# A hybrid decoder block on one Trainium2 core: weights split in their own order, a ring that waits for whole quads only from expert 9, and the final norm's rows made at expert 22

## The chip, the cores and the metric

The kernel runs on one core of one Trainium2 chip. The metric is the device time of one launch in microseconds (us). The kernel before was timed three times: 1261.85, 1260.22 and 1263.72 us, median 1261.85. One execution more was profiled; its own time was 1259.29 us, and the span that the profiler shows of it 1257.5 us.

## The reference

The input is 256 tokens of width 1024; 16 learned meta tokens are put ahead of them. All is fp32.

```python
hn = rmsnorm(h, norm_mix)                                   # mixer
u, q, k, v, g_ssm, g_attn = split(hn @ w_in)                # 1024 1024 128 128 1024 1024
ssm_out = z * sigmoid(z @ w_glu + b_glu),  z = gelu(s5(u))  # diagonal recurrence, 64 groups x 64 states
attn_out = window_attention(rotary(q), rotary(k), v, sinks) # window 128, 16 heads, 2 kv heads
mix = sigmoid(g_ssm) * (ssm_out @ w_br_ssm) + sigmoid(g_attn) * (attn_out @ w_br_attn)
h = h + mix @ w_out
h = h + moe(rmsnorm(h, norm_ffn))                           # top 4 of 32 experts
return rmsnorm(h, norm_final)[:, 16:]
# moe, for each token and each of its 4 experts e, weighted by the softmax of the top-4 logits:
g, up = split(x @ w_gate_up[e] + b_gate_up[e])              # 1024 -> 2 x 1024
y = (min(g, 7) * sigmoid(1.702 * g) * (clip(up, -7, 7) + 1)) @ w_down[e] + b_down[e]
```

The weights of one expert are 12 MiB (8 of gate_up, 4 of down), so the 32 experts read 384 MiB from HBM.

## The kernel before

**Two halves.** The first 331 us are the mixer: the norm, the blocks of w_in, the recurrence, and then a loop over `n` (its body ends at L1265) in which 40 blocks of weights pass through a pipeline: `gate` (n 0 to 7), `glu`, `ssm`, `attn` and `out`, eight each. A block's weights (128 x 1024) are split in two parts: `hi` (L927, ACT) writes the high part `wh`, `lo` (L929 to L930, DVE or POOL) the rest `wl`; `mm` (L944 to L953, PE) multiplies three times; `e1` to `e4` work on the result. The 14 steps of the attention (maxima, exponentials, normalisation, transposes, values) are woven into the passes n = 0 to 13. The rest of the span is the router and the loop over the 32 experts `e` (L1552).

**The lists' order.** The experts' down weights and the residual `xt` use an order in which 512 columns, seen as 128 x 4, are turned to 4 x 128. `reorder(t, q)` (L903 to L906) turns a quarter of the residual, by two copies on POOL through a free piece of `late_`, at n = 3, 4, 5 and 6. The out blocks are split with a strided read (`self.p`, L924 to L930), and so come out in that order; `e2` (L974 to L979) adds the residual on DVE in PSUM and ACT copies the sum to `xt`; `e3` (L987) squares it; `turn_out` (L994 to L1002) turns it by eight matmuls with the identity, 64 wide, for the router. At the other end `down` (L1441 to L1442) evacuates PSUM with a strided read, `combine` (L1467) adds to `acc`, and `scale` (L1528 to L1529) turns the result back by strided operations on ACT and DVE.

**The ring.** The experts' weights come through `Ring` (L131 to L165), on SP's DMA queue. It owns slots of 1 MiB: four quads, which the trace names by the tile they lie in (`r`, `ZScgtX`, `QYWgt`, `ws`), and slots that stand alone (one in `r`, one in `aA`). A unit of work is 4 MiB; it goes out as one transfer to a whole free quad, as halves of 2 MiB, or as single slots. Slots come free when PE has used them, and each release calls `pump`. With `patient` set, a unit that has not begun waits for a whole quad and everything behind it waits too. That is set by one line in the loop over the experts:

```python
ring.patient, ring.most = 4 < e < 29, 4 if e < 29 else 2
```

**The end.** At the last expert ACT's queue loads the rows of `norm_final` (L1556) and PE spreads them over the partitions into two PSUM banks (`nf_banks`, L1508 to L1511), which `weigh` (L1524) and `scale` read; `squares` and `root` (L1516 to L1520) make the norm, and three of SP's transfers and one of ACT's write the output (L1531 to L1532).

Of the kernel before, what the change touches and what calls it, by code (L numbers as in the profile page):

```python
# [95 lines left out]
class Ring:  # L96
# [36 lines left out]
    def pump(self):  # L133
        while self.free and self.todo:
# [11 lines left out]
            row = self.room(4) if left == self.most else None  # L146
# [57 lines left out]
def hybrid_block(ctx: ExitStack, tc: tile.TileContext, x, meta, norm_mix, w_in, lam_re, lam_im, log_dt,  # L204
# [698 lines left out]
    def reorder(t, q):  # L903
        v, tmp = xt[:, t, 512 * q:512 * q + 512], late_[:, 3 * 512:]
        G.tensor_copy(tmp, v)
        G.tensor_copy(v.rearrange("p (c n) -> p c n", c=4), tmp.rearrange("p (n c) -> p c n", c=4))  # L906

    class Block:
# [5 lines left out]
        def hi(self):  # L914
# [48 lines left out]
        def e2(self):  # L963
# [10 lines left out]
            elif self.kind == "out" and self.h:  # L974
                pu = pus[self.i][:, :, :256].rearrange("p t (c n) -> p t c n", c=4)
                for t in range(2):
                    V.scalar_tensor_tensor(pu[:, t], pu[:, t], 0.5, strips(t, self.i), op0=OP.mult, op1=OP.add)
                for t in range(2):
                    S.activation(strips(t, self.i), pu[:, t], AF.Copy)  # L979
# [223 lines left out]
    for n in range(B + 2):  # L1203
# [33 lines left out]
        if 3 <= n < 7:  # L1237
            reorder((n - 3) // 2, (n - 3) % 2)
# [18 lines left out]
        if n == 22:  # L1257
            ring.slots([aA(8 * L + 768, U_)])
# [157 lines left out]

    cols2 = lambda t: t.rearrange("p (n c) -> p c n", c=4)
    rows2 = lambda t: t.rearrange("p (c n) -> p c n", c=4)

    def down(hT_, wc, selr, y, odd, mid=None, two=False):  # L1420
# [20 lines left out]
        S.activation(rows2(y[:64, odd]), cols2(py[0][:64]), AF.Copy)  # L1441
        V.tensor_copy(rows2(y[64:, 1 - odd]), cols2(py[1][64:]))  # L1442
# [18 lines left out]
    def combine(gT, y, then=None):  # L1461
        for t in range(2):
            for hf in range(2):
# [3 lines left out]
                V.tensor_tensor(acc[:, t, cs_], (acc if started else xt)[:, t, cs_], pc, op=OP.add)  # L1467
# [232 lines left out]
```

## Time and profile before

| what | before |
|---|---|
| median of three runs | 1261.85 us |
| the profiled execution, its span | 1259.29 us, 1257.5 us |
| PE busy | 1186.2 us (94%) |
| DVE, ACT, POOL busy | 461.9, 235.7, 65.0 us |
| bytes moved | 447.26 MB, mean 356 GB/s |
| chain that ended last | PE 64%, DMA 26%, DVE 7%, ACT 2% |

The chain is followed back from the last instruction, so its shares say which engine or transfer was waited for. The mean of 356 GB/s mixes a mixer that moves less than 240 GB/s over most of its time with experts at about 432. A row of the timeline gives the start, the duration, the engine, the line, the output and inputs, and in square brackets the idle time before it and what ended it.

### The profile page before, as it was taken

The numbers are of one execution on the slowest core, as the hardware profiler recorded it, in microseconds if no ns is written. First come the engines' busy times: TensorE is split into PE (matmuls) and PEld (weight loads), VectorE is DVE, ScalarE is ACT, GpSimd is POOL, SyncE is SP. The second block draws the span as 40 slices with busy tenths as digits, with TensorE's granted clock in tenths as the row PEclk, the third lists the DMA queues.
The fourth block names the chain that finished last, engine by engine and source line by source line (L and its number), as shares of the span: only waits on it lengthen the run. The fifth ranks groups of instructions, "written<-read, shape, count | busy, mean of one in ns | idle before, by whom it ended". The sixth has DMA issues, their size and how long they took to land.

```text
span 1257.5 us, 16838 instructions
## 1 busy us (share of the span) xinstructions
PE 1186.2 (94%) x7200; PEld 598.1 (48%) x7201; DVE 461.9 (37%) x1002; ACT 235.7 (19%) x478; POOL 65.0 (5%) x97
## 2 busy tenths in 40 slices
PE   8989979999899999999999989899998989999995
PEld 6878768899533333333333333333332333333331
DVE  4979467778421222322121212222231312121223
ACT  3353456647100000000000000000000000000002
POOL 3019130000000000000000000000000000000000
PEclk9999989999999999999999999999999999999998
DMA  7934345685889999999999999999999999999993
GB/s 181 238 84 140 131 149 170 135 318 208 366 358 431 427 430 386 433 433 433 432 432 433 431 432 433 432 430 432 432 433 432 431 432 433 430 431 432 426 430 146
DMA packets 76401, 447.26 MB, mean 356 GB/s; under 512 B 22377, under 2 KB 58461, under 8 KB 59937
## 3 DMA queue, kind: packets, MB, share of 16 engines
q1 hardware_dynamic: 75660, 445.40, 87.3%
q8 instruction: 59, 0.97, 0.3%
q0 software_dynamic: 512, 0.45, 0.2%
q10 hardware_dynamic: 148, 0.27, 0.1%
q14 instruction: 22, 0.17, 0.0%
HBM read 443.32 MB, written 2.79 MB: 355 GB/s over the span
## 4 chain that ended last, share of the span: by engine, by line
PE 64%; DMA 26%; DVE 7%; ACT 2%; issue 1%; POOL 0%; SPq 0%; DVEq 0%; ACTq 0%
PE pgt L1390 13%; PE pup L1390 11%; PE py L1435 11%; DMA ZScgtX<-in_w_gate_up_dram 10%; DMA r<-in_w_gate_up_dram 10%; PE pg L1363 6%; PE pc L1465 4%; PE pu L506 2%; DMA QYWgt<-in_w_gate_up_dram 2%; PE pu L951 2%; DMA r<-in_w_down_dram 2%; PE pu L952 2%; PE pu L953 2%; PE pu L496 2%; PE pt L1411 1%
## 5 line engine op out<-in xcount | busy, mean ns | idle before, releaser
L1364 DVE TENSOR_TENSOR xw<-pg,nfB 128x256 f32<-128x256 f32 x64 | 27.2, 425 | 223.4 <-PE pg L1363 223.4
L1401 DVE TENSOR_SCALAR gs<-pgt 128x512 f32<-128x512 f32 x32 | 22.0, 687 | 212.4 <-PE pgt L1390 212.4
L1363 PEld LDWEIGHTS pg<-aA,xt 128*128 128x128 f32 x512 | 62.7, 193 | 57.2 <-issue 56.0
L1442 DVE COPY late__1943<-py 64x512 f32<-64x512 f32 x32 | 22.2, 694 | 169.7 <-ACT late__1943 L1441 167.4
L1390 PE MATMUL pgt<-r,xw 128*64 128x512 f32 x272 | 73.4, 618 | 9.1 <-DMA r<-in_w_gate_up_dram 9.1
L1363 PE MATMUL pg<-aA,xt 128*128 128x128 f32 x512 | 74.6, 289 | 2.5 <-DVE aA L1353 2.2
L1390 PE MATMUL pgt<-ZScgtX,xw 128*64 128x512 f32 x256 | 68.3, 612 | 7.2 <-DMA ZScgtX<-in_w_gate_up_dram 7.2
L1390 PE MATMUL pup<-r,xw 128*64 128x512 f32 x272 | 72.6, 612 | 0.0
L951 PE MATMUL pu<-kr,wh 128*128 128x256 f32 x240 | 69.3, 289 | 0.0
L1435 PE MATMUL py<-ws,hT 128*64 128x512 f32 x272 | 61.9, 607 | 7.1 <-DMA ws<-in_w_down_dram 7.0
L953 PE MATMUL pu<-kr,wl 128*128 128x256 f32 x240 | 67.4, 281 | 0.2 <-DVE wl L930 0.2
L1390 PE MATMUL pup<-ZScgtX,xw 128*64 128x512 f32 x256 | 67.4, 606 | 0.0
L952 PE MATMUL pu<-kr,wh 128*128 128x256 f32 x240 | 67.4, 281 | 0.0
L1435 PE MATMUL py<-QYWgt,hT 128*64 128x512 f32 x260 | 61.2, 621 | 6.5 <-DMA QYWgt<-in_w_down_dram 6.5
L1390 PE MATMUL pgt<-QYWgt,xw 128*64 128x512 f32 x240 | 63.4, 607 | 0.8 <-DMA QYWgt<-in_w_gate_up_dram 0.8
L1413 ACT ACTIVATE hT<-pt 128x512 f32<-128x512 f32 x32 | 19.1, 597 | 231.4 <-PE pt L1411 231.4
L1390 PE MATMUL pup<-QYWgt,xw 128*64 128x512 f32 x240 | 61.6, 592 | 0.0
L1390 PE MATMUL pgt<-ws,xw 128*64 128x512 f32 x232 | 61.3, 607 | 0.0
L1441 ACT ACTIVATE late__1943<-py 64x512 f32<-64x512 f32 x32 | 18.9, 591 | 223.2 <-PE py L1435 223.2
L1390 PE MATMUL pup<-ws,xw 128*64 128x512 f32 x232 | 59.5, 592 | 0.0
L1465 PE MATMUL pc<-late__1943,gT 128*128 128x512 f32 x120 | 58.3, 618 | 0.0
L1380 ACT ACTIVATE gT<-pt 128x512 f32<-128x512 f32 x16 | 9.6, 597 | 256.0 <-PE pt L1379 256.0
(363 smaller groups left out, 1780.1 us busy)
## 6 DMA issues: line engine op xcount, KB each, us to landing
ZScgtX<-in_w_gate_up_dram SPq DMA_DIRECT2D x12, 4096.0 KB
ws<-in_w_gate_up_dram SPq DMA_DIRECT2D x12, 4096.0 KB
QYWgt<-in_w_gate_up_dram SPq DMA_DIRECT2D x12, 4096.0 KB, 29.2
r<-in_w_gate_up_dram SPq DMA_DIRECT2D x11, 4096.0 KB
ws<-in_w_down_dram SPq DMA_DIRECT2D x7, 4096.0 KB, 15.7
QYWgt<-in_w_down_dram SPq DMA_DIRECT2D x6, 4096.0 KB, 24.5
r<-in_w_down_dram SPq DMA_DIRECT2D x6, 4096.0 KB
ZScgtX<-in_w_down_dram SPq DMA_DIRECT2D x6, 4096.0 KB
```

The source lines that it names most:

```text
L496: T.matmul(pu[:, t], x_[:, 4 * self.h + k, c:c + 128], y_[:, k], start=(self.h + t + p + k == 0), skip_group_check=True, stop=(self.h == 1 ...
L506: T.matmul(pu, x_[:, k], y_[:, k, c:], start=(p + k == 0), stop=(p == len(pairs) - 1 and k == 7))
L951: T.matmul(pu, self.a[:, k], hi[:, k], start=(k == 0), stop=False)
L952: T.matmul(pu, self.a[:, k], lo[:, k], start=False, stop=False)
L953: T.matmul(pu, self.b[:, k], hi[:, k], start=False, stop=(k == 7))
L1363: T.matmul(pg[:, j], xt[:, t, 128 * (k + j):128 * (k + j) + 128], oh[:, t], start=(t == 0), stop=(t == 1))
L1364: V.tensor_tensor(xe[:, k:k + 2], pg, nfB[:, k:k + 2, None].to_broadcast([128, 2, n]), op=OP.mult)
L1390: T.matmul(p_[64 * hf:64 * hf + 64].rearrange("p (n c) -> p n c", c=4), lhs, half_of(rhs[:, c:c + D], hf), start=False, stop=(k == 7), til ...
L1401: V.tensor_scalar(gv, turned(pg), LIMIT, None, op0=OP.min)
L1435: T.matmul(py[pp][64 * pp:64 * pp + 64], lhs, rhs[:, 512 * hf:512 * hf + 512], start=(c == -1), stop=(c == 7), tile_position=(0, 64 * pp), ...
L1442: V.tensor_copy(rows2(y[64:, 1 - odd]), cols2(py[1][64:]))
L1465: T.matmul(pc, gT[:, hf, t], y[:, hf], start=True, stop=True)
```

## The change

**The ring.** A unit takes a whole quad only if all its four pieces are left, single slots standing alone are used for an even piece only if two of them are free, and an odd piece takes any free slot. Patience for whole quads begins at e = 9 in place of 5. At e = 9 the slot `aA(8 * L + 768)` is taken out of the ring; its memory is used below.

**The reorder.** It moves from n = 3 to 6 to n = 17 to 20, and its first copy, now the strided one, from POOL to ACT; POOL copies back contiguously.

**The out blocks.** Their weights are split straight. `e2` reads PSUM strided and writes the sum in the lists' order to a new SBUF tile `xo`; the squares read `xo`; ACT copies `xo` to `xt` after them; and `turn_out` is four 128-wide transposes of `xo`.

**The experts' sums.** PSUM is evacuated straight, the first combine (e = 3) turns the residual by a strided add, so that `acc` stands in the model dimension's own order, and the final scale is straight.

**The final norm's rows.** `norm_rows` (two small transfers on ACT's queue, two matmuls, two copies by ACT into SBUF) runs at e = 22, in place of `nf_banks` and of the load at e = 31.

SP's instructions for experts 5 to 9 of the weight stream, before; a row is a transfer, with its destination and the width of a partition's row in elements (2048 is a slot, 8192 a quad):

```order
L162 DMA QYWgt<-in_w_down_dram 128x4096
L162 DMA ZScgtX<-in_w_down_dram 128x4096
L162 DMA ZScgtX<-in_w_gate_up_dram 128x4096
L162 DMA ws<-in_w_gate_up_dram 128x4096 x2
L162 DMA r_63<-in_w_gate_up_dram 128x4096
L162 DMA QYWgt<-in_w_down_dram 128x8192
L162 DMA ZScgtX<-in_w_gate_up_dram 128x8192
L162 DMA ws<-in_w_gate_up_dram 128x8192
L162 DMA r_63<-in_w_down_dram 128x8192
```

The same place of the changed kernel (`L1606` loads the largest count of an expert's rows, once, after expert 8):

```order
L162 DMA r_63<-in_w_gate_up_dram 128x4096
L162 DMA QYWgt<-in_w_down_dram 128x4096
L162 DMA r_63<-in_w_down_dram 128x4096
L162 DMA QYWgt<-in_w_gate_up_dram 128x4096
L162 DMA ZScgtX<-in_w_gate_up_dram 128x4096
L162 DMA aA<-in_w_gate_up_dram 128x2048
L162 DMA r_63<-in_w_gate_up_dram 128x2048
L1606 TENSOR_LOAD imax
L1606 ISA x2
L162 DMA ZScgtX<-in_w_gate_up_dram 128x4096
L162 DMA ws<-in_w_down_dram 128x8192
L162 DMA r_63<-in_w_gate_up_dram 128x8192
```

The first whole quad was a down unit into `QYWgt`, at the beginning of expert 5; it is now a down unit into `ws`, after expert 8, and halves and single slots stand before it.

POOL's instructions from the last weight part that it makes to the router, before:

```order
L930 TENSOR_TENSOR wl<-r_63,wh 128x1024
L905 COPY late__1943<-xt 128x512
L906 COPY xt<-late__1943 128x512
L905 COPY late__1943<-xt 128x512
L906 COPY xt<-late__1943 128x512
L905 COPY late__1943<-xt 128x512
L906 COPY xt<-late__1943 128x512
L905 COPY late__1943<-xt 128x512
L906 COPY xt<-late__1943 128x512
L1288 TENSOR_TENSOR rs_3775<-aA,nhalf 128x2
```

ACT's instructions of the changed kernel at n = 17 to 20, where the first copy of each quarter (`xr`) now stands:

```order
L925 ACTIVATE wh<-r_63 128x1024 x2
L905 ACTIVATE xr<-xt 128x512
L925 ACTIVATE wh<-r_63 128x1024
L905 ACTIVATE xr<-xt 128x512
L1222 ACTIVATE kr<-aA 128x512 x2
L925 ACTIVATE wh<-r_63 128x1024
L905 ACTIVATE xr<-xt 128x512
L1222 ACTIVATE kr<-aA 128x512 x2
L925 ACTIVATE wh<-aA 128x1024
L905 ACTIVATE xr<-xt 128x512
L925 ACTIVATE wh<-aA 128x1024
```

POOL's eight copies became four, each of which waits for one of these ACT copies, and stand between the passes of the `ssm` blocks.

PE's instructions from the end of the last out block to the first ones of the router, before (`pu` are the router's logits, `L364` fills a pause):

```order
L944 MATMUL sc<-wh,kr 128x256
L945 MATMUL sc<-wl,kr 128x256
L946 MATMUL sc<-wh,kr 128x256
L1008 MATMUL pu<-wr,aA 128x32 x4
L1000 MATMUL pt<-ct,xt 64x128 x8
L1008 MATMUL pu<-wr,aA 128x32 x4
L364 LDWEIGHTS b_1453
L364 MATMUL pt<-b_1453 128x416
```

The same instructions of the changed kernel:

```order
L942 MATMUL sc<-wh,kr 128x256
L943 MATMUL sc<-wl,kr 128x256
L944 MATMUL sc<-wh,kr 128x256
L1006 MATMUL pu<-wr,aA 128x32 x4
L999 MATMUL pt<-ct,xo 128x128 x4
L1006 MATMUL pu<-wr,aA 128x32 x4
L364 LDWEIGHTS b_1453
L364 MATMUL pt<-b_1453 128x416
```

The transposes read `xo`, which DVE writes, where the matmuls read `xt`, which ACT wrote after DVE; there are four in place of eight.

The diff, cut to what is spoken of:

```diff
@@ Ring.pump
             left = u.n - u.at
-            row = self.room(4) if left == self.most else None
+            row = self.room(4) if left == 4 == self.most else None
             if row is None and left == 4 and self.patient:
                 return
             if row is None and left > 1 and u.at % 2 == 0:
                 row = self.room(2)
-            if row is None and alone:
+            if row is None and len(alone) > 1 - u.at % 2:
                 row = alone[:1]
-            if row is None and left == 1 and u.n == 1:
-                row = self.free[:1]
+            if row is None and (u.at % 2 or u.n == 1):
+                row = (alone or self.free)[:1]
@@ reorder
-        v, tmp = xt[:, t, 512 * q:512 * q + 512], late_[:, 3 * 512:]
-        G.tensor_copy(tmp, v)
-        G.tensor_copy(v.rearrange("p (c n) -> p c n", c=4), tmp.rearrange("p (n c) -> p c n", c=4))
+        v, tmp = xt[:, t, 512 * q:512 * q + 512], pools["pa"].tile([128, 512], F32, tag="xo", name="xr", bufs=1)
+        S.activation(tmp.rearrange("p (c n) -> p c n", c=4), v.rearrange("p (n c) -> p c n", c=4), AF.Copy)
+        G.tensor_copy(v, tmp)
@@ Block.hi, Block.lo
-            S.activation(self.p(self.a), self.v, AF.Copy)
+            self.v = v
+            S.activation(self.a, self.v, AF.Copy)
...
-            eng.tensor_tensor(self.p(self.b), self.v, self.p(self.a.bitcast(F32)), op=OP.subtract)
+            eng.tensor_tensor(self.b, self.v, self.a.bitcast(F32), op=OP.subtract)
@@ Block.e2, e3, turn_out (out blocks)
-                    V.scalar_tensor_tensor(pu[:, t], pu[:, t], 0.5, strips(t, self.i), op0=OP.mult, op1=OP.add)
-                for t in range(2):
-                    S.activation(strips(t, self.i), pu[:, t], AF.Copy)
+                    V.scalar_tensor_tensor(self.x[:, t].rearrange("p (c n) -> p c n", c=4), pu[:, t], 0.5,
+                                           strips(t, self.i), op0=OP.mult, op1=OP.add)
...
+                for t in range(2):
+                    S.activation(strips(t, self.i), self.x[:, t].rearrange("p (c n) -> p c n", c=4), AF.Copy)
...
-                        for c in range(2):
-                            T.matmul(pt[64 * c:64 * c + 64, 128 * t:128 * t + 128], strips(t, self.i)[:, 2 * (k % 2) + c],
-                                     ident, start=True, stop=True, tile_position=(0, 64 * c), skip_group_check=True)
+                        T.transpose(pt[:, 128 * t:128 * t + 128], self.x[:, t, 128 * (k % 2):128 * (k % 2) + 128], ident)
@@ the loop over n
-        if 3 <= n < 7:
-            reorder((n - 3) // 2, (n - 3) % 2)
+        if 17 <= n < 21:
+            reorder((n - 17) // 2, (n - 17) % 2)
@@ down, combine
-        S.activation(rows2(y[:64, odd]), cols2(py[0][:64]), AF.Copy)
-        V.tensor_copy(rows2(y[64:, 1 - odd]), cols2(py[1][64:]))
+        S.activation(y[:64, odd], py[0][:64], AF.Copy)
+        V.tensor_copy(y[64:, 1 - odd], py[1][64:])
...
+                    own = lambda v: v.rearrange("p (n c) -> p c n", c=4)
+                    V.tensor_tensor(own(acc[:, t, cs_]), xt[:, t, cs_].rearrange("p (c n) -> p c n", c=4), own(pc), op=OP.add)
@@ norm_rows, scale
+    def norm_rows():
+        nfr = aA(8 * L + 768 + D, 512)
         for hf in range(2):
-            T.matmul(rows2(nf[hf]), cv["ones"][32 * hf:32 * hf + 1], cols2(nfr[32 * hf:32 * hf + 1]), start=True, stop=True)
-        return nf
+            S.dma_start(out=nfr[32 * hf:32 * hf + 1], in_=norm_final[512 * hf:512 * hf + 512].rearrange("(o d) -> o d", o=1))
+        for hf in range(2):
+            pn = bank("t", "nf")
+            T.matmul(pn, cv["ones"][32 * hf:32 * hf + 1], nfr[32 * hf:32 * hf + 1], start=True, stop=True)
+            S.activation(nfb[:, 512 * hf:512 * hf + 512], pn, AF.Copy)
...
-        S.activation(cols2(o[:, :512]), rows2(spare[t][:, :512]), AF.Copy, scale=rsf[:, t:t + 1])
-        V.scalar_tensor_tensor(cols2(o[:, 512:]), rows2(acc[:, t, 512:]), rsf[:, t:t + 1], rows2(nf[1]),
-                               op0=OP.mult, op1=OP.mult)
+        S.activation(o[:, :512], spare[t][:, :512], AF.Copy, scale=rsf[:, t:t + 1])
+        V.scalar_tensor_tensor(o[:, 512:], acc[:, t, 512:], rsf[:, t:t + 1], nfb[:, 512:], op0=OP.mult, op1=OP.mult)
@@ the loop over e
+                if k == 1 and e == max(0, n_exp - 10):
+                    norm_rows()
...
+            if e == 9:
+                ring.retire(s_n)
-            ring.patient, ring.most = 4 < e < 29, 4 if e < 29 else 2
+            ring.patient, ring.most = 8 < e < 29, 4 if e < 29 else 2
```

## Rows read from the trace of the kernel before

**Rows 1.** The page's second part: the span in 40 slices of 31.4 us, GB/s moved.

```profile
GB/s 181 238 84 140 131 149 170 135 318 208 366 358 431 427 430 386 433 433 433 432 432 433 431 432 433 432 430 432 432 433 432 431 432 433 430 431 432 426 430 146
```

**Rows 2.** What PE waited for in 560 to 1147 us: total us, times, longest.

```profile
PE pgt L1390 <- DMA ZScgtX<-in_w_gate_up_dram: 7.2, 5, 2.1
```

**Rows 3.** The timeline of PE in the last expert.

```profile
1228.64 0.66 PE L1411 MATMUL pt<-ct,gs 128*128 128x128 f32 x4
...
1233.79 1.94 PE L1435 MATMUL py<-r,hT 128*64 128x512 f32 x8 [0.69 <-DMA r<-in_w_down_dram]
```

**Rows 4.** The timeline of SP's DMA queue at the beginning of expert 5.

```profile
459.84 0.33 SPq L162 DMA_DIRECT2D r<-in_w_gate_up_dram  x1
482.92 0.33 SPq L162 DMA_DIRECT2D QYWgt<-in_w_down_dram  x1
```

**Rows 5.** Stretches: busy us of PE, PEld, DVE, ACT, POOL; granted clock, DMA share, GB/s.

```profile
364.00:480.00 116.00, 115.78 (x560) 44.00 (x558) 29.97 (x65) 9.10 (x16) 0.00 (x0) 1.00 1.01 429
480.00:482.00 2.00, 2.00 (x12) 0.70 (x10) 1.57 (x3) 0.26 (x1) 0.00 (x0) 1.00 0.67 287
482.00:484.00 2.00, 2.00 (x12) 0.56 (x8) 0.51 (x1) 0.00 (x0) 0.00 (x0) 1.00 0.30 82
484.00:486.00 2.00, 2.00 (x12) 0.68 (x10) 0.00 (x0) 0.00 (x0) 0.00 (x0) 1.00 0.85 213
600.00:800.00 200.00, 187.53 (x875) 69.83 (x873) 45.22 (x93) 14.18 (x24) 0.00 (x0) 0.98 1.00 433
```

**Rows 6.** The timeline of POOL beside the attention.

```profile
167.31 1.33 POOL L906 COPY xt<-late__1943 128x512 f32<-128x512 f32 x1
```

**Rows 7.** The timeline of DVE between two steps of the attention.

```profile
155.40 0.69 DVE L1074 TENSOR_TENSOR ZScgtX<-ZScgtX 128x512 f32<-128x512 f32 x1
...
167.70 1.48 DVE L1074 TENSOR_TENSOR ZScgtX<-ZScgtX 128x512 f32<-128x512 f32 x1
171.70 1.74 DVE L1026 TENSOR_TENSOR aA<-aA 128x768 f32<-128x768 f32 x1 [2.52 <-ACT aA L1024]
173.37 0.56 DVE L1152 TENSOR_TENSOR sm<-sm 112x2 f32<-112x2 f32 x1
...
174.16 1.41 DVE L1154 TENSOR_TENSOR late__1943<-late__1943,sm 112x480 f32<-112x480 f32 x1
...
179.80 0.96 DVE L1026 TENSOR_TENSOR aA<-aA 128x768 f32<-128x768 f32 x1 [2.21 <-ACT aA L1024]
180.68 0.15 DVE L1152 TENSOR_TENSOR sm<-sm 112x2 f32<-112x2 f32 x1
...
181.06 0.66 DVE L1154 TENSOR_TENSOR late__1943<-late__1943,sm 112x480 f32<-112x480 f32 x1
```

**Rows 8.** What PE waited for in 160 to 200 us.

```profile
PE pt L1176 <- DVE late__1943 L1154: 5.3, 1, 5.3
```

**Rows 9.** The timeline of ACT at the end.

```profile
1247.89 0.61 ACT L1516 ACTIVATE sq<-aA 128x512 f32<-128x512 f32 x1
...
1248.57 2.53 ACT L1528 ACTIVATE QYWgt<-QYWgt,rsf 128x512 f32<-128x512 f32 x2
```

**Rows 10.** What ACT waited for at n = 17 to 21.

```profile
ACT wh L927 <- PE pu L952: 8.9, 7, 1.7
```

**Rows 11.** Who waited for line 930, the split's second step, in the whole span.

```profile
  PEld sc L945: 0.4, 2
```

**Rows 12.** The timeline of PE behind the last out block.

```profile
322.66 1.15 PE L1000 MATMUL pt<-ct,xt 128*64 128x128 f32 x16 [0.66 <-ACT xt L979]
```

**Rows 13.** The timeline of ACT behind the last out block.

```profile
322.22 0.66 ACT L979 ACTIVATE xt<-sc 128x256 f32<-128x256 f32 x2 [6.27 <-DVE sc L977]
```

**Rows 14.** Line 1441, the evacuation of PSUM by ACT, in the whole span.

```profile
L1441 ACT ACTIVATE late__1943<-py x32: 591/591/592, 378.7 to 1243.3; 64x512 f32<-64x512 f32 x32
```

**Rows 15.** The timeline of DVE at the end.

```profile
1249.12 2.07 DVE L1529 SCALAR_TENSOR_TENSOR QYWgt<-aA,rsf,nf 128x512 f32<-128x512 f32 x2
```

**Rows 16.** The stretch after PE's wait, columns as in rows 5.

```profile
174.00:179.00 5.00, 3.28 (x13) 2.87 (x14) 3.49 (x8) 2.33 (x8) 1.05 (x1) 0.50 0.02 3
```

More of the change, by code (lines that the diff above doesn't have):

```diff
@@ L923, in hi @@
                 self.b = pools["pa"].tile(sh, F32R, tag="wl", name="wl", bufs=2)
-            self.v, self.p = v, lambda t: t
-            if self.kind == "out":
-                self.v, self.p = v.rearrange("p k (n c) -> p k c n", c=4), lambda t: t.rearrange("p k (c n) -> p k c n", c=4)
-            S.activation(self.p(self.a), self.v, AF.Copy)
+            self.v = v
+            S.activation(self.a, self.v, AF.Copy)
         def lo(self, eng=V):
-            eng.tensor_tensor(self.p(self.b), self.v, self.p(self.a.bitcast(F32)), op=OP.subtract)
+            eng.tensor_tensor(self.b, self.v, self.a.bitcast(F32), op=OP.subtract)
             if self.h:
@@ L974, in e2 @@
             elif self.kind == "out" and self.h:
[L975 removed]
+                pu = pus[self.i][:, :, :256].rearrange("p t (n c) -> p t c n", c=4)
+                self.x = pools["pa"].tile([128, 2, 256], F32, tag="xo", name="xo", bufs=1)
                 for t in range(2):
[L977 to L979 removed]
+                    V.scalar_tensor_tensor(self.x[:, t].rearrange("p (c n) -> p c n", c=4), pu[:, t], 0.5,
+                                           strips(t, self.i), op0=OP.mult, op1=OP.add)
         def e3(self):
@@ L1257, in hybrid_block @@
         if n == 22:
-            ring.slots([aA(8 * L + 768, U_)])
+            s_n = ring.slots([aA(8 * L + 768, U_)])[0]
         if n == 24:
@@ L1466, in combine @@
                 cs_ = slice(512 * hf, 512 * hf + 512)
-                V.tensor_tensor(acc[:, t, cs_], (acc if started else xt)[:, t, cs_], pc, op=OP.add)
+                if started:
+                    V.tensor_tensor(acc[:, t, cs_], acc[:, t, cs_], pc, op=OP.add)
+                else:
+                    own = lambda v: v.rearrange("p (n c) -> p c n", c=4)
+                    V.tensor_tensor(own(acc[:, t, cs_]), xt[:, t, cs_].rearrange("p (c n) -> p c n", c=4), own(pc), op=OP.add)
                 if then:
@@ L1520, in root, with weigh, scale, last @@
         G.tensor_tensor(rsf[:, t:t + 1], ssf[:, t, 0:1], nhalf, op=OP.pow)
-    def weigh(t, nf):
-        V.tensor_tensor(spare[t][:, :512], acc[:, t, :512], nf[0], op=OP.mult)
-    def scale(t, nf):
+    def weigh(t):
+        V.tensor_tensor(spare[t][:, :512], acc[:, t, :512], nfb[:, :512], op=OP.mult)
+    def scale(t):
         o = spare[t][:, D:]
-        S.activation(cols2(o[:, :512]), rows2(spare[t][:, :512]), AF.Copy, scale=rsf[:, t:t + 1])
-        V.scalar_tensor_tensor(cols2(o[:, 512:]), rows2(acc[:, t, 512:]), rsf[:, t:t + 1], rows2(nf[1]),
-                               op0=OP.mult, op1=OP.mult)
+        S.activation(o[:, :512], spare[t][:, :512], AF.Copy, scale=rsf[:, t:t + 1])
+        V.scalar_tensor_tensor(o[:, 512:], acc[:, t, 512:], rsf[:, t:t + 1], nfb[:, 512:], op0=OP.mult, op1=OP.mult)
         (S if t else nc.sync).dma_start(out=ov[:, t, :512], in_=o[:, :512])
         nc.sync.dma_start(out=ov[:, t, 512:], in_=o[:, 512:])
-    def last(nf):
+    def last():
         for t in range(2):
             root(t)
-            weigh(t, nf)
-            scale(t, nf)
+            weigh(t)
+            scale(t)
     groups = {e: min(2, n_exp - e) for e in range(0, n_exp, 2)}
@@ L1549, in hybrid_block @@
     imax = cp.tile([128, 1], I32, name="imax")
-    more, nf = None, []
+    more = None
     for e in range(n_exp + 1):
         f = e - 1
-        if e == n_exp - 1:
-            nfr = pm.tile([128, 512], F32, tag="gT", name="nfr", bufs=3)
-            for hf in range(2):
-                S.dma_start(out=nfr[32 * hf:32 * hf + 1], in_=norm_final[512 * hf:512 * hf + 512].rearrange("(o d) -> o d", o=1))
         if e < n_exp:
@@ L1565, in mid @@
                     combine(GT.pop(e - 3), Y.pop(e - 3))
-                if k == 4 and e == n_exp - 1:
-                    nf.extend(nf_banks())
+                if k == 1 and e == max(0, n_exp - 10):
+                    norm_rows()
                 if k in (0, 3, 5, 6, 7) or e == 0:
                     next(pend, None)
-            ring.patient, ring.most = 4 < e < 29, 4 if e < 29 else 2
+            if e == 9:
+                ring.retire(s_n)
+            ring.patient, ring.most = 8 < e < 29, 4 if e < 29 else 2
             HID[e] = gate_up(lambda k: XE[e][:, k], ring_w, gate_up_bias(selrow(e)) if e else bias0, mid)
@@ L1614, in sums @@
         for tt in range(2):
-            weigh(tt, nf)
+            weigh(tt)
         root(1)
         for tt in range(2):
-            scale(tt, nf)
+            scale(tt)
     assert list(GT) == [n_exp - 2]
@@ L1665, in hybrid_block @@
                 squares(t, hf)
-        last(nf)
+        last()
     close(hp2)
```

8 lines of the change are left out of this document (2 added, 6 removed).

## The prediction

> **What bounds the kernel now.** I read the throughput by slices first, then the stretches, the waits of PE and of SP's queue, and last the timelines at the places that the change touches. The slices [rows 1] show two kernels in one. Up to slice 10 (314 us) the DMA engines move 84 to 318 GB/s: the mixer is bound by the engines. From slice 13 on they move about 432, flat, but for slice 16 (471 to 503 us, 386): the experts are bound by the stream of weights. PE's waits agree: between 560 and 1147 us it waits for transfers again and again; one source of the four is in [rows 2], 7.2 us in five waits. So an engine's microsecond saved among the experts is worth nothing before the last transfer has landed, at 1233.8 us, where PE takes up a piece of the last down weights after waiting 0.69 us for it [rows 3]. A microsecond saved in the mixer, on its chain, starts the stream earlier: from 336 us on the transfers go out as PE releases slots, so it is worth a whole one at the end. And a hole in the stream costs what did not flow.
>
> The sum is made against the profiled execution, 1259.29 us. The median of the three runs, 1261.85, is 2.6 above it, and I add that at the end.
>
> **The ring, the hole at expert 5.** SP issues nothing from 459.84 to 482.92 us, 23.1 us [rows 4]: patience has begun and no quad is whole. The stream runs dry: 287, 82 and 213 GB/s in three stretches of 2 us, against 433 later [rows 5]. What is lost is 2 x (146 + 351 + 220) / 433 = 3.3 us. Patience from expert 9 removes this hole: **-3.3**. What is late next is the hole that the same rule could tear at expert 9. At expert 5 the queue lasted from 459.84 to about 481.3 (287 of 433 in the stretch from 480), 21.5 us or 8.9 MiB. Since PE is busy 187.53 of 200 us where the stream is flat [rows 5], a pair of experts, 24 MiB or 58.1 us of stream, costs PE only 54.5 us, so PE frees slots 3.6 us earlier by each pair. Two pairs later the queue has 7.2 us more in it, 28.7 us. A pause as long as that at expert 5, 23.1 us, fits into it. I take 0, with 0 to 3.3 as bounds.
>
> **The ring, halves in place of quads.** Experts 5 to 8, twelve units, now come in halves and some single slots, 50.3 MB in at least twelve transfers more. Halves with a few singles run at 429 GB/s, quads at 433 [rows 5]: 117.3 against 116.2 us, **+1.1**. The bounds are 0 and 24 us, by the rival on transfers below. That fewer single slots go out in the last experts I count at nothing.
>
> The Trainium skill ("SBUF — State Buffer", section "The DMA setup-cost knee") says that each transfer pays a roughly fixed 2 us, which gives 4 MiB transfers a higher rate than 1 MiB ones. By it, twelve transfers more would make an estimated +24 us in place of +1.1. The row at 429 GB/s speaks against adding such prices up while several transfers are under way.
>
> **The reorder leaves POOL's old place.** While POOL copies [rows 6], DVE's instructions on the chain of the attention take longer than the same ones a step earlier or later [rows 7]: L1074 1.48 against 0.69, L1026 1.74 against 0.96, L1152 0.56 against 0.15, L1154 1.41 against 0.66. The excess is 0.79 + 0.78 + 0.41 + 0.75 = 2.7 us. L1154 is what PE then waits 5.3 us for [rows 8], and ACT and DVE go on with the next steps right behind it. All four are on that chain: **-2.7**. Bounds 0 (the bias transfers on the queues at the same time, and not POOL, made them slow) and -2.7.
>
> **Its new place.** At n = 17 to 20 ACT makes four strided copies, POOL four straight ones. A strided ACT instruction of this size takes 2.53 / 2 = 1.26 us, a straight one 0.61 [rows 9]. ACT waits there 8.9 us for PE in seven waits [rows 10], 1.27 a pass, just what a copy takes; and PE is never short of ACT or DVE in that part. So the copies fill ACT's idle time: 0. Without that cover each pass would have 1.26 us on ACT and 1.33 of a POOL copy [rows 6] in the way, 4 x 2.59 = 10.4; that is the upper bound.
>
> **The out blocks.** The split of a straight read is shorter on both engines; what PE felt of the strided one is two short waits, 0.4 in all [rows 11]: **-0.4**. `turn_out` takes 1.15 us on PE as eight matmuls [rows 12], four transposes of the same kind 0.66 [rows 3]: 0.49 less, three times where PE is the bound: **-1.5**. Behind the last block PE waits 0.66 for ACT's copy [rows 12, 13], which the transposes no longer need, and they are 0.49 shorter. From this 1.15 I take off 0.35, for a dependence on DVE's second half remains: **-0.8**. Together bounds of 0 and -3.1. The first combine adds strided in place of straight; were each of its four adds to double as ACT's copy does, some 2.6 us would fall where PE has 3.6 us of slack a pair: 0. The straight evacuations save nothing on the path, for the same reason.
>
> For PSUM, the Trainium skill ("Advanced Engine Details and Errata", section "Memory Cachelines") says that two fp32 values make a line and that non-contiguous patterns slow matmuls significantly. If that held for DVE's now strided reading in `e2`, the last block would have an estimated 0.9 more and the gain would be 0.9 smaller. Here ACT reads PSUM with stride 4 in 0.59 us [rows 14], no more than the 0.61 of a straight read of SBUF [rows 9], so I add nothing.
>
> **The final norm.** Its matmuls leave the last expert, whose end the last transfer sets: 0. At expert 22 the two small transfers queue among weights; PE has slack there, and their wait is bounded by 0 and by one pair's 3.6 us. I take 0. The final scale becomes straight: ACT's pair takes 2.53 us and would take 1.22, but DVE's pair beside it ends last and shrinks less, from 2.07 [rows 15] to about 1.4 (L1154's 0.66 for 480 columns [rows 7], for 512 twice): **-0.65**, bounds 0 and -1.3.
>
> **Sum.** Mixer -2.7 - 0.4 - 1.5 - 0.8 = -5.4; ring -3.3 + 1.1 = -2.2; end -0.65. That is -8.25, so 1251.0 for an execution like the profiled one, and **1253.6 us** as a median. Its own range is 1251 to 1256.
>
> **Rivals.**
> *The mixer's gain stays out.* DVE was slow for the bias transfers, or PE's own work after the attention absorbs what is saved. For it: DMA was busy near there. Against: DVE is fast again as soon as POOL has stopped. Without the 2.7: 1256.3. Chance 0.10.
>
> *The hole moves to expert 9.* Then the change does not do what it says: the 3.3 stay, 1256.9. For it: the rule and the ring's size are the same. Against: the 28.7 us of queue. Chance 0.08.
>
> *The clock gives back too.* After PE's idle 5.3 us the granted clock is 0.50, the 1.2 GHz level, while PE is busy 3.28 us [rows 8, 16]. With PE idle only about 2.6 us it might stay at 2.4 GHz, and 1.6 us of PE's work would go: 1252.0. Against: that work lies beside ACT's and DVE's chain. Chance 0.12.
>
> *The moved copies are in the way.* ACT's idle time was filled to the brim, so PE waits at n = 17 to 20: +10.4, which leaves 1264.0, not told from no change. It decides from 8.25 us on. Chance 0.04.
>
> *Each transfer has a price of its own.* After a dry queue data comes about 2 us after the issue [rows 4, 5]. If every transfer paid this, twelve more would cost 24 us: 1253.6 - 1.1 + 24 = 1276.5, slower. The price from which the gain is gone is 9.35 / 12 = 0.8 us. Against: the 429 GB/s in halves [rows 5]. Chance 0.03. The Trainium skill's fixed 2 us, named above, is the same figure; by its rule this rival would hold.
>
> **How the numbers follow.** The forecast has the remaining 0.63. A measurement of this kernel tells 0.3%, 3.8 us, from no change, so faster means under 1258.1. The forecast and the first three rivals lie below it, 0.93; for two of them meeting, or a run 2 us higher, I take off 0.06. Faster 0.87, within 0.3% 0.09 (the moved copies and those), slower 0.04. The range takes in the two rivals at 1256.3 and 1256.9 and, below, the clock with the bounds at the end: 1249.5 to 1257.5.
>
> **What would show it.** Right: SP has no pause over 15 us at expert 5 and no slice below 425 GB/s from 13 to 38; L1026 and L1154 take 0.96 and 0.66 us in both steps; PE's wait at L1176 is about 2.6 us; the last block's transposes follow DVE at once; the experts' first matmul comes some 5 us earlier; each of DVE's last scales takes 0.7. Wrong: a hole at 560 to 600 us, PE waits for ACT or POOL at n = 17 to 20, a rate under 425 in 364 to 560, or DVE still slow at 170 us with POOL idle.

## The result, and the profile after

The changed kernel took 1250.70 us in the median of four runs (1250.1 to 1253.0), the kernel before 1262.28 beside it; the ratio of the two kernels is put at 0.9921, with a 95% interval of 0.9907 to 0.9936. By this ratio that is 10.0 us less (8.1 to 11.7), where 8.25 were forecast and 1253.6 us as the median. The quotient of the two medians alone is 0.9908, or 11.6 us, and lies inside the interval. Two more sets of five runs gave 1250.52 and 1250.04 us. The range of 1249.5 to 1257.5 held the time.

The first trace of the changed kernel is that of its slowest execution, 1253.0 us. It shows more of the lower clock ahead of the experts than the third trace, of 1248.9 us. I take the first where the clock plays no part and the third for sums. The span of the third is 1247.1 us, 10.4 less than before.

**The ring.** The page's GB/s of the first trace, to be read against [rows 1]:

```profile
GB/s 182 239 85 138 134 161 160 139 316 264 299 404 429 430 431 426 432 431 431 435 434 430 430 432 431 435 432 428 432 434 433 429 430 431 435 431 432 426 428 140
```

The 16th slice, which begins at 469 us here, has 426 where the hole stood at 386. SP's queue at the places of the old and of the new beginning of patience:

```profile
456.79 0.33 SPq L162 DMA_DIRECT2D r<-in_w_gate_up_dram  x1
460.96 0.33 SPq L162 DMA_DIRECT2D QYWgt<-in_w_down_dram  x1
469.60 0.33 SPq L162 DMA_DIRECT2D r<-in_w_down_dram  x1
475.52 0.33 SPq L162 DMA_DIRECT2D QYWgt<-in_w_gate_up_dram  x1
...
568.56 0.34 SPq L162 DMA_DIRECT2D ZScgtX<-in_w_gate_up_dram  x1
581.38 0.33 SPq L162 DMA_DIRECT2D ws<-in_w_down_dram  x1
595.09 0.33 SPq L162 DMA_DIRECT2D r<-in_w_gate_up_dram  x1
```

The longest pause at expert 5 is 8.6 us, against 23.1 in [rows 4]. At expert 9, behind 559 us, there are pauses of 12.8 and 13.7 us. The stretches of the same trace, columns as in [rows 5]:

```profile
355.00:475.00 120.00, 119.47 (x576) 45.48 (x576) 30.61 (x64) 8.82 (x15) 0.00 (x0) 1.00 1.00 427
480.00:482.00 2.00, 2.00 (x12) 0.69 (x10) 0.00 (x0) 0.00 (x0) 0.00 (x0) 1.00 1.06 446
482.00:484.00 2.00, 2.00 (x14) 0.65 (x12) 0.06 (x1) 0.59 (x1) 0.00 (x0) 1.00 0.94 401
484.00:486.00 2.00, 2.00 (x12) 0.68 (x10) 0.63 (x1) 0.00 (x0) 0.00 (x0) 1.00 0.99 426
560.00:580.00 20.00, 18.45 (x76) 7.72 (x77) 5.29 (x14) 0.60 (x1) 0.00 (x0) 0.91 1.01 431
580.00:600.00 20.00, 20.00 (x104) 7.72 (x102) 5.75 (x14) 1.71 (x3) 0.00 (x0) 1.00 1.02 437
```

At expert 9 the stream goes on at 431 and 437 GB/s: those pauses are covered by what the queue held. Bytes summed over stretches of the third trace and of the one before, shifted by 6 us, put the stream 0.4 us ahead at 460, 3.6 at 480 and 2.9 at 535: the ring gave 2.5. How much of it is the hole and how much the halves is not shown. The drop from 3.6 to 2.9 lies wholly in the 15 us right behind the hole, in which the kernel before moved more than its flat rate, as if catching up (the third trace, then the one before):

```profile
480.00:495.00 15.00, 15.00 (x74) 5.12 (x72) 1.31 (x2) 1.19 (x2) 0.00 (x0) 1.00 1.00 426
```

```profile
486.00:501.00 15.00, 15.00 (x74) 5.10 (x72) 1.26 (x2) 1.19 (x2) 0.00 (x0) 1.00 1.04 445
```

From 495 to 555, where halves still go out, the lead is 2.9 at both ends.

**The reorder.** DVE beside the attention, to be read against [rows 7], first trace:

```profile
168.56 0.69 DVE L1072 TENSOR_TENSOR ZScgtX<-ZScgtX 128x512 f32<-128x512 f32 x1
171.76 0.96 DVE L1024 TENSOR_TENSOR aA<-aA 128x768 f32<-128x768 f32 x1 [2.51 <-ACT aA L1022]
172.64 0.15 DVE L1150 TENSOR_TENSOR sm<-sm 112x2 f32<-112x2 f32 x1
...
173.03 0.66 DVE L1152 TENSOR_TENSOR late__1943<-late__1943,sm 112x480 f32<-112x480 f32 x1
```

L1072 (before L1074), L1024 (L1026), L1150 (L1152) and L1152 (L1154) have their short durations. A fifth instruction was slow beside POOL's first copy, and the forecast does not count it; here it is in the kernel before, and once more a step later:

```profile
166.74 0.53 DVE L1141 TENSOR_SCALAR sm<-sm 112x2 f32<-112x2 f32 x1
...
176.37 0.17 DVE L1141 TENSOR_SCALAR sm<-sm 112x2 f32<-112x2 f32 x1
```

With its 0.36 the excess was 3.1 us. One instruction of this chain is still slow, beside POOL's part of a weight split, which the change left where it was (third trace):

```profile
164.68 2.40 POOL L928 TENSOR_TENSOR wl<-r,wh 128x1024 fp32r<-128x1024 f32 x1 [34.31 <-ACT wh L925]
```

```profile
165.03 2.08 DVE L1138 TENSOR_TENSOR sm<-sm,snk 112x2 f32<-112x2 f32 x1
```

It ends when POOL's instruction ends, and a step later it takes 0.16 us. No kernel moved that split, so what it would give is open.

PE's longest wait for L1152 is 1.7 us, 2.5 in two, against 5.3 [rows 8]. ACT and POOL at n = 17 to 19, the new place:

```profile
249.65 1.12 ACT L905 ACTIVATE xr<-xt 128x512 f32<-128x512 f32 x1
251.49 1.06 ACT L925 ACTIVATE wh<-r 128x1024 fp32r<-128x1024 f32 x1 [0.73 <-ACT xr L905]
```

```profile
250.83 0.61 POOL L906 COPY xt<-xr 128x512 f32<-128x512 f32 x1 [82.92 <-ACT xr L905]
253.65 0.61 POOL L906 COPY xt<-xr 128x512 f32<-128x512 f32 x1 [2.21 <-ACT xr L905]
```

The strided copy takes 1.12 us, POOL's 0.61 (0.96 and 0.76 in the last two quarters), and ACT is idle for 0.73 us behind the first, which the view puts down to the copy itself. In 200 to 332 us PE waits for neither.

**The out blocks.** PE behind the last block, to be read against [rows 12], third trace:

```profile
316.29 0.80 PE L999 MATMUL pt<-ct,xo 128*128 128x128 f32 x4
317.46 1.08 PE L1006 MATMUL pu<-wr,aA 128*128 128x32 f32 x8 [0.36 <-DVE aA L1000]
```

There is no wait for ACT any more; 0.36 us of one for DVE has come behind the transposes. From the attention's first product with the values into `QYWgt` on PE (L1187 at 190.81, L1189 at 193.50 before) to the start of this L1006 it is 126.65 us in the third trace and 130.46 before (L1008 at 323.96): 3.8 less.

**The end.** POOL's two roots in the third trace, DVE's two scales, and before them the same roots in the trace before:

```profile
1237.60 0.93 POOL L1525 TENSOR_TENSOR rsf<-ssf,nhalf 128x1 f32<-128x1 f32 x1 [917.73 <-DVE ssf L1524]
1238.91 0.98 POOL L1525 TENSOR_TENSOR rsf<-ssf,nhalf 128x1 f32<-128x1 f32 x1 [0.39 <-DVE ssf L1524]
```

```profile
1242.94 0.74 DVE L1534 SCALAR_TENSOR_TENSOR QYWgt<-aA,rsf 128x512 f32<-128x512 f32 x1
1244.12 0.75 DVE L1534 SCALAR_TENSOR_TENSOR QYWgt<-aA,rsf 128x512 f32<-128x512 f32 x1 [0.44 <-POOL rsf L1525]
```

```profile
1247.97 0.56 POOL L1520 TENSOR_TENSOR rsf<-ssf,nhalf 128x1 f32<-128x1 f32 x1 [921.56 <-DVE ssf L1519]
1249.28 0.55 POOL L1520 TENSOR_TENSOR rsf<-ssf,nhalf 128x1 f32<-128x1 f32 x1 [0.75 <-DVE ssf L1519]
```

The scales take 0.74 and 0.75 in place of 2.07 for both [rows 15]; but the roots take 0.93 and 0.98 in place of 0.56 and 0.55, and the second scale waits 0.44 us for POOL (in the first trace, from which DVE's rows are). From PE's last combine to the end of the span it is 13.4 us in the third trace (1233.74 to 1247.1) and 13.4 before (1244.12 to 1257.5). The straight scale gained nothing.

What the norm's rows cost at expert 22, first trace:

```profile
PE nf L1516 <- DMA aA<-in_norm_final_dram: 3.2, 2, 1.8
```

These 3.2 us (3.9 in the third trace, a little over the forecast's bound of 3.6) lie where PE has slack. Behind them the granted clock falls to its lower level, 0.50 from 950 to 955 us in the first trace. The slices there, 30 to 32, still have 434, 433 and 429 GB/s.

**The sum from the traces.** Third trace against the one before: the experts' first matmul at 324.55 in place of 331.03 (-6.5: up to PE's L1187 in the attention -2.7, the rest of the mixer -3.8), the stream behind expert 9 another 2.5 ahead, and PE's last wait for a transfer at 1223.41 in place of 1233.79:

```profile
1223.41 1.94 PE L1429 MATMUL py<-ws,hT 128*64 128x512 f32 x8 [1.02 <-DMA ws<-in_w_down_dram]
...
1233.74 1.99 PE L1445 MATMUL pc<-late__1943,gT 64*128 64x512 f32 x8 [0.82 <-DVE late__1943 L1436]
```

That last is -10.4, so another 1.4 came in the experts behind, most of it in the last ones: at 1200 us the stream is 9.1 ahead. From PE's last combine to the end of the span it is even. This 1.4 is no firm figure. From the experts' first matmul to PE's last combine (L1445, L1451 before) it is 913.1 us in the trace before, 912.8 and 912.5 in those of experiments 3 and 4, which have the ring of before, 911.0 in experiment 2, and 910.4, 909.9 and 909.2 in the first, second and third trace of the changed kernel. Executions of one kernel differ by 1.2 us in it, and the third is the shortest.

### The profile page after: what moved, and what is told of

Same layout as the page of the kernel before. It is cut to its first block, busy times and chain, and to the rows that moved or that the text cites. A ratio compares the mean times of both kernels' runs of the same rounds, so it can differ in the third digit from the quotient of the medians.

```text
span 1251.2 us, 16784 instructions
## 1 busy us (share of the span) xinstructions
PE 1185.1 (95%) x7152; PEld 599.3 (48%) x7153; DVE 450.3 (36%) x1002; ACT 231.8 (19%) x484; POOL 60.8 (5%) x93
## 4 chain that ended last, share of the span: by engine, by line
PE 71%; DMA 21%; DVE 5%; ACT 2%; issue 1%; POOL 0%; ACTq 0%; SPq 0%; DVEq 0%; POOLq 0%
PE pgt L1388 14%; PE py L1429 13%; PE pup L1388 13%; DMA ZScgtX<-in_w_gate_up_dram 10%; DMA r<-in_w_gate_up_dram 6%; PE pg L1361 6%; PE pc L1459 4%; PE pu L506 4%; DMA ws<-in_w_down_dram 3%; PE pu L949 2%; PE pu L951 2%; PE pu L950 2%; PE pu L496 2%; PE pt L1409 1%; PE sc L1038 1%
## 5 line engine op out<-in xcount | busy, mean ns | idle before, releaser
L1429 PE MATMUL py<-ws,hT 128*64 128x512 f32 x312 | 70.9, 605 | 6.0 <-DMA ws<-in_w_down_dram 6.0
L1388 PE MATMUL pgt<-QYWgt,xw 128*64 128x512 f32 x264 | 70.3, 612 | 0.0
L1388 PE MATMUL pup<-QYWgt,xw 128*64 128x512 f32 x264 | 68.7, 599 | 0.0
L1429 PE MATMUL py<-ZScgtX,hT 128*64 128x512 f32 x240 | 53.3, 593 | 2.1 <-DMA ZScgtX<-in_w_down_dram 2.1
L1388 PE MATMUL pgt<-ws,xw 128*64 128x512 f32 x208 | 55.0, 608 | 0.0
L1462 DVE TENSOR_TENSOR aA<-aA,pc 128x512 f32<-128x512 f32 x56 | 38.5, 687 | 45.9 <-PE pc L1459 45.9
```

Source lines behind the costliest of these rows:

```text
L1388: T.matmul(p_[64 * hf:64 * hf + 64].rearrange("p (n c) -> p n c", c=4), lhs, half_of(rhs[:, c:c + D], hf), start=False, stop=(k == 7), til ...
L1429: T.matmul(py[pp][64 * pp:64 * pp + 64], lhs, rhs[:, 512 * hf:512 * hf + 512], start=(c == -1), stop=(c == 7), tile_position=(0, 64 * pp), ...
L1462: V.tensor_tensor(acc[:, t, cs_], acc[:, t, cs_], pc, op=OP.add)
```

## The experiments

Each time comes with its ratio to the kernel before, which ran beside it on the same chip. A gain in us is taken from this ratio; where it bears on the argument, the difference of the two medians stands beside it.

**1. The changed kernel again.** No edit.

> The changed kernel once more. In its first trace the granted clock was 0.50 from 321 to 327 us, in the router, and the gather's 16 matmuls took 3.74 us in place of 2.05. Theory A: the fall belongs to that one execution (1253.0 us, the slowest of four); then this trace has 1.00 there, the experts' first matmul at 325.9 in place of 327.55, and a span 1.7 shorter. Theory B: the fall comes from the change, which took idle time of PE ahead of the router away; then it is at 0.50 again and the runs at 1250.1 to 1250.7 are faster for another reason. Ratio to the kernel before 0.992 in both.

1250.52 us, ratio 0.9922 (0.9910 to 0.9935). The gather, in this trace and in the first:

```profile
323.54 2.02 PE L1361 MATMUL pg<-aA,xt 128*128 128x128 f32 x16 [0.84 <-DVE aA L1351]
```

```profile
323.88 3.74 PE L1361 MATMUL pg<-aA,xt 128*128 128x128 f32 x16 [0.51 <-DVE aA L1351]
```

The clock is at full here, and the first matmul of the experts at 325.49. Theory A holds: the fall belongs to the execution, for one and the same kernel has it or has it not. The traces of kernels 2, 3 and 4 below, each with a part of the change, have it too.

**2. The ring alone**, on the kernel before:

```diff
-            row = self.room(4) if left == self.most else None
+            row = self.room(4) if left == 4 == self.most else None
...
-            ring.patient, ring.most = 4 < e < 29, 4 if e < 29 else 2
+            ring.patient, ring.most = 8 < e < 29, 4 if e < 29 else 2
```

and the two rules for single slots as in the change.

> The kernel before with the ring's rules and patience from expert 9 alone; all else as before. Theory: the hole of 3.3 us at 482 goes and halves cost 0.6 to 1.1, so the time falls by 2.2 to 2.7 us (ratio 0.9979 to 0.9983). Rival (the hole moves to expert 9): 0, ratio 1.000. Rival (each transfer has its price): slower by some us.

1258.08 us, ratio 0.9976 (0.9967 to 0.9985): -3.0 us (-1.9 to -4.2; 2.6 by the medians). The stretches at the old hole and at expert 9, columns as before:

```profile
482.00:484.00 2.00, 2.00 (x14) 0.87 (x12) 1.58 (x6) 0.32 (x1) 0.00 (x0) 1.00 0.95 410
...
475.00:500.00 25.00, 25.00 (x125) 9.51 (x126) 6.38 (x15) 2.30 (x4) 0.00 (x0) 1.00 1.01 431
...
560.00:600.00 40.00, 37.74 (x182) 14.80 (x180) 12.65 (x29) 2.49 (x5) 0.00 (x0) 1.00 1.01 431
```

410 where 82 stood, and 431 at expert 9. The hole did not move.

**3. The reorder alone**, on the kernel before:

```diff
-        if 3 <= n < 7:
-            reorder((n - 3) // 2, (n - 3) % 2)
+        if 17 <= n < 21:
+            reorder((n - 17) // 2, (n - 17) % 2)
```

with ACT's strided and POOL's straight copy through a tile of its own.

> The kernel before with the reorder moved to n = 17 to 20 (ACT's strided and POOL's straight copy) alone. Theory (POOL's copies slow DVE on the attention's chain): L1026, L1154 take 0.96 and 0.66 us at 171 and 173, and the time falls by 2.7 to 3.9 us (ratio 0.9969 to 0.9979). Rival (bias transfers slow DVE): DVE is as slow as before and the time the same. Rival (the copies are in the way at n = 17 to 20): up to 10.4 slower.

1258.51 us, ratio 0.9979 (0.9970 to 0.9988): -2.6 us (-1.5 to -3.8; 2.2 by the medians). The bias transfers are those of the kernel before, and DVE is fast:

```profile
164.48 0.66 DVE L1139 TENSOR_REDUCE sm<-sc 112x2 f32<-112x480 f32 x1 [2.68 <-issue]
...
172.43 0.66 DVE L1154 TENSOR_TENSOR late__1943<-late__1943,sm 112x480 f32<-112x480 f32 x1
```

```profile
191.03 0.59 PE L1189 MATMUL pu<-QYWgt,aA 128*64 128x448 f32 x1
```

From the first row's reduction to PE's L1189 it is 26.55 us; before it was 29.63 (163.87 to 193.50). POOL's copies were the cause, at 3.1 us here, which is the excess of the five slow instructions. The step itself began 0.6 us later (164.48); why is not shown.

**4. The out blocks alone**, on the kernel before (straight split, sum in `xo`, four transposes):

```diff
-            S.activation(self.p(self.a), self.v, AF.Copy)
+            S.activation(self.a, self.v, AF.Copy)
...
+                        T.transpose(pt[:, 128 * t:128 * t + 128], self.x[:, t, 128 * (k % 2):128 * (k % 2) + 128], ident)
```

> The kernel before with the changed out blocks alone (straight split, sum in SBUF, four transposes). Theory: 2.7 us less (0.4 of waits, 1.5 of turning, 0.8 behind the last block), ratio 0.9979, all of it between 285 and 324 us. Rival (these steps lie beside other work): 0 to -1.

1257.93 us, ratio 0.9970 (0.9961 to 0.9980): -3.8 us (-2.5 to -4.9; 2.8 by the medians), though this trace had the fall in the router. PE's turning of one block and the next logits, here and before:

```profile
309.13 0.60 PE L999 MATMUL pt<-ct,xo 128*128 128x128 f32 x4
...
312.41 0.97 PE L1006 MATMUL pu<-wr,aA 128*128 128x32 f32 x8
```

```profile
309.27 1.09 PE L1000 MATMUL pt<-ct,xt 128*64 128x128 f32 x16
...
313.24 0.97 PE L1008 MATMUL pu<-wr,aA 128*128 128x32 f32 x8
```

From the turning to the next logits it is 3.28 us here and 3.97 before: 0.69 a block, where 0.49 was counted. From one turning to the next it is 7.00 us here (302.13 to 309.13) and 7.79 before (301.48 to 309.27), 0.79 less. The next matmuls begin 0.35 us behind the first transpose and 1.02 behind the first of eight matmuls. From the first matmul of the out blocks to the last block's second logits it is 28.1 us here and 31.6 before: the trace has 3.5.

**5. The norm's rows in PSUM**, on the changed kernel: PE spreads the rows into two PSUM banks in the last expert, and no longer at expert 22.

```diff
-            S.activation(nfb[:, 512 * hf:512 * hf + 512], pn, AF.Copy)
...
-        V.tensor_tensor(spare[t][:, :512], acc[:, t, :512], nfb[:, :512], op=OP.mult)
+        V.tensor_tensor(spare[t][:, :512], acc[:, t, :512], nf[0], op=OP.mult)
...
+                if k == 4 and e == n_exp - 1:
+                    nf.extend(nf_banks())
```

> The changed kernel, but the norm's rows are spread by PE into two PSUM banks in the last expert, as before (straight now), and weigh and scale read them there; the small loads stay at expert 22. Theory: with the rows in SBUF, DVE's weigh and scale have two SBUF inputs, POOL's two roots beside them take 0.94 and 0.99 us in place of 0.56 and 0.55, and ACT and DVE wait for POOL at the second half; this ate the 0.65 expected of the straight scale. Then POOL takes 0.55 again and the stretch from PE's last combine to the end of the span, 13.27 and 13.35 in two profiles of the changed kernel and 13.38 before, is 12.7 to 12.8; ratio to the changed kernel 0.9995. Rival: the end was bound elsewhere (the output's transfers): it stays 13.3.

1251.70 us, ratio 0.9932 (0.9914 to 0.9950). POOL's roots:

```profile
1240.87 0.56 POOL L1530 TENSOR_TENSOR rsf<-ssf,nhalf 128x1 f32<-128x1 f32 x1 [919.72 <-DVE ssf L1529]
1242.18 0.55 POOL L1530 TENSOR_TENSOR rsf<-ssf,nhalf 128x1 f32<-128x1 f32 x1 [0.75 <-DVE ssf L1529]
```

0.56 and 0.55 again, and 12.9 us from the last combine (1237.01) to the end of the span (1249.9), in place of 13.3 to 13.4. It is 12.9 to 13.0 in all three kernels with the rows in PSUM (5, 8 and 11), and 13.3 to 13.4 in all six traces with them in SBUF. The mechanism is shown, at 0.4 us rather than 0.6; the runs scatter by more than that, and the median shows no gain.

**6. More filling in the router**, on the changed kernel:

```diff
-    keep_clock(bank("y", "idle"), b3[:, :128], b3[:, :416], 2)
+    keep_clock(bank("y", "idle"), b3[:, :128], b3[:, :416], 3)
...
-    keep_clock(bank("y", "idle"), b3[:, :128], b3[:, :416], 2)
+    keep_clock(bank("y", "idle"), b3[:, :128], b3[:, :416], 4)
```

> The changed kernel with 1 and 2 more filling matmuls in the two pauses of the router (3 and 4 in place of 2 and 2). Theory: the granted clock falls in the router when PE's idle pieces add up there; filled, it stays at 1.00 from 316 to 328, the gather's 16 matmuls take 2.05 us, and the median falls by up to 1 us (two of three executions of these kernels had the fall, at 1.7 each). Rival: the fall does not depend on the pauses; the gather takes 3.7 us in this profile too, or the time is the same.

1250.74 us, ratio 0.9926 (0.9908 to 0.9943). The gather took 2.02 us and the clock stayed, but the median is no lower: inconclusive by itself.

**7. Never patient**, on the changed kernel:

```diff
-            ring.patient, ring.most = 8 < e < 29, 4 if e < 29 else 2
+            ring.patient, ring.most = 32 < e < 29, 4 if e < 29 else 2
```

> The changed kernel with patience never set, so that units go out in halves and single slots up to expert 28 too (some 60 units more than in the changed kernel). Theory (the ring's term): experts 5 to 8 lost 0.6 us by it, 0.15 an expert, so 20 experts more lose 3 us, ratio to before about 0.9945, and the rate is 428 to 430 GB/s throughout. Rival (each transfer has a price of about 2 us, or half of it): 60 to 120 us slower.

1254.30 us, ratio 0.9950 (0.9932 to 0.9967), 3.6 above kernel 6 beside it and 2.6 above kernel 5. Two stretches:

```profile
600.00:800.00 200.00, 191.66 (x904) 69.91 (x900) 46.35 (x96) 14.21 (x24) 0.00 (x0) 1.00 1.01 430
800.00:1000.00 200.00, 190.35 (x882) 69.02 (x882) 48.87 (x101) 15.29 (x26) 0.00 (x0) 0.99 1.01 429
```

430 and 429 GB/s, against 432 in both stretches of the third trace, with quads. There are 200 transfers of weights in place of 141; the 59 more cost 3.6 us, 0.06 each, not 2.

**8. Both**, rows in PSUM and more filling.

> Both: the norm's rows in PSUM and the filling. If both theories hold, 0.6 and up to 1 us less than the changed kernel, about 1249.2 where that has 1250.5, ratio to before 0.991; if neither, 0.992.

1249.34 us, ratio 0.9916 (0.9898 to 0.9934); no fall in the router, and 12.95 us from the last combine to the end.

**9. No filling in the router**, on the changed kernel (both lines of experiment 6 left out).

> The changed kernel without the filling matmuls of the router's two pauses (0 in place of 2 and 2). Theory (the clock falls there when PE's idle pieces add up): the granted clock is at 0.50 from about 322 to 328 or longer, the gather takes 3.6 us or more, and the median is 0.3 to 1 us above the changed kernel's on the same chip. Rival (the fall doesn't depend on the pauses): the gather is at full clock, or the median the same.

1251.83 us (1251.23 to 1253.73), ratio 0.9933 (0.9919 to 0.9946). The clock in the router:

```profile
321.00:327.00 6.00, 4.31 (x21) 3.85 (x22) 2.41 (x10) 0.05 (x1) 0.00 (x0) 0.50 0.99 426
```

It is 0.50 for six microseconds, and the gather takes 3.75. The median is more above the changed kernel's than the 0.3 to 1 us expected (experiment 10).

**10. The changed kernel a third time**, beside kernels 9 and 11.

> The changed kernel a third time, beside the other two of this call: 0.992 to the kernel before; its trace shows once more whether the clock falls in the router (it did in one of two).

1250.04 us (1248.80 to 1250.47), ratio 0.9915 (0.9901 to 0.9928), no fall in the router. All its runs lie under all of kernel 9's: the filling is worth 1.8 us by the medians.

**11. Both, again.**

> Rows in PSUM and more filling, on the same chip as the changed kernel: 0.4 us less for the end, and no fall of the clock in the router, which is worth up to 1.7 us in an execution where the changed kernel has one. The median is 0.4 to 1.5 us under the changed kernel's. Rival: the fall comes in spite of the filling, the median is within 0.4.

1248.64 us (1248.36 to 1249.87), ratio 0.9908 (0.9895 to 0.9922), 1.4 under kernel 10 on the same chip; the runs of the two overlap. It is the fastest version that ran, and faster than the kernel before; that it beats the changed kernel is likely (both times lower) but not beyond the scatter.

## Why the prediction was right

The time lay in the range, 2.9 us under the forecast, and the mechanisms of the three large terms were the ones named. Of the 2.9 some 1.2 lie in the base: the forecast stands on a median of 1261.85 from three runs, and 27 later runs put the kernel before at 1260.68. The rest is the sum of misses both ways, so that the total is closer than its terms: more from the out blocks, nothing from the scale.

| term | forecast | alone, from the ratio | alone, from the medians | from the traces |
|---|---|---|---|---|
| ring: hole -3.3, halves +1.1 | -2.2 | -3.0 | -2.6 | -2.5 |
| reorder off the attention | -2.7 | -2.6 | -2.2 | -2.7 |
| out blocks | -2.7 | -3.8 | -2.8 | -3.8 |
| last experts | 0 | not run | not run | -1.4, not firm |
| straight scale | -0.65 | not run | not run | 0 |
| sum | -8.25 | -9.4 for the three | -7.5 for the three | -10.4 |

*The hole* went as worked out, though its 3.3 was summed over stretches that end before the stream's catching up; the step on expert 9 held, with pauses of 14 us, shorter than the 23.1 that were granted to it. *The halves* have no price of their own in these traces. Experiment 7 lost 3.6 us by halves and single slots in 20 experts; from this, four would cost an estimated 0.7, two thirds of what was counted. *The reorder*: the mechanism was right, and the sum left out L1141, so that 3.1 us came back in the stretch itself. At PE's L1187 2.7 of them are left, since the step began 0.4 us later in the third trace: that the forecast's 2.7 is met so closely is luck. *Its new place* cost nothing. *The out blocks* were mis-sized. "0.49 less, three times" took the durations of the groups; the distance to the next group is what counts, and it fell by 0.69, 2.05 for three. From the last block's first logits to its second ones it was 0.95 (2.93 before, 1.98 in the third trace) in place of 0.8. From the first matmul of the blocks to the first turning, where the split's waits were, it was 0.6 in place of 0.4. These are 3.6 of the 3.8; the other 0.2 lie between a block's logits and the next turning, 0.1 in each of two blocks. The runs of experiment 4 alone do not tell 2.7 from 3.8; the traces do.

*The straight scale* is the step that failed: "DVE's pair beside it ends last and shrinks less" left POOL out. The rows of the norm moved to SBUF with the change, so DVE's weighing and scaling read two operands there, and POOL's roots beside them became 0.4 us longer, each; the second half of the output waits for the second root. Experiment 5 moved the rows back to PSUM, and the roots' 0.55 us and 0.4 us of the end came back with them. *The last experts*: that fewer single slots go out was counted at nothing, and PE's last wait came 1.3 us earlier in the third trace than the stream's lead at 1200 us explains. Experiment 2 has that rule with the rest of the ring, and its experts are 2.1 us shorter than before, no more than the ring's own term; executions of the changed kernel differ by 1.2. So nothing shows that the rule gave anything, and the cause stays open.

The rivals: the gain of the mixer did not stay out (experiment 3), the hole did not move (2), the copies were in no one's way (3), and transfers have no price of their own near 2 us (7). On the clock the forecast looked in the wrong place. After the attention it still falls in the third trace, and experiment 3, without that fall, takes the same 26.55 us from the reduction to PE: off the path, as argued. But in the router, where no rival had it, it comes and goes from execution to execution, at up to 1.7 us. With two filling matmuls in each pause six of nine traces have it, with three and four none of three, without any the one that there is; by luck alone three of three would be one in 27.

For PSUM, DVE's strided reading cost nothing here: L976, which writes to SBUF, took 412 to 425 ns in the first trace, L977 before, which read straight and wrote to PSUM, 431 to 433. The rule of the Trainium skill ("Advanced Engine Details and Errata", section "Memory Cachelines") speaks of matmuls; carried over to DVE's reading, it would have taken an estimated 0.9 us from the gain, and the trace shows none of it. The fixed price of a transfer that the Trainium skill names ("SBUF — State Buffer", section "The DMA setup-cost knee") does not add up here over transfers that queue: by experiment 7 one more cost 0.06 us.

## What to carry to other kernels

Read a slow instruction beside the same instruction a step earlier: where it doubles only while another engine copies, moving the copy to a place where its engine waits anyway gave the excess back whole. List every instruction beside the copy, the short ones too. In a stream-bound stage, price a rule of issue by the longest pause that it makes against what the queue holds, not by the number of transfers. Size what a group of PE instructions costs by the distance to the next group's start, and when an operand moves from PSUM to SBUF, look at which engine works beside its reader.

## What the runs showed of the hardware

POOL's [128x1] power took 0.55 us beside DVE instructions with an operand in PSUM and 0.93 to 0.99 beside the same ones with both in SBUF. A [112x2] DVE instruction took 2.08 us beside a POOL subtraction of 2.40 us, ending with it, and 0.16 a step later. A transfer more, in halves and single slots of 1 to 2 MiB in a full queue, cost 0.06 us. The granted clock in one and the same kernel fell to the lower level at different places in different executions, ahead of the experts at 160 to 167, 174 to 178 or 320 to 328 us. The fall at 174 to 178 left the way through the attention at 26.55 us; the one in the router put up to 1.7 us on the gather.
